# Another order of the seven products of the down projection in a one-core encoder block, with the last norm and the outputs set elsewhere in it

## The chip, the cores and the metric

The kernel runs on one core of a Trainium2 chip. The metric is the device time of one execution in microseconds, from the hardware. The time before is the median of three runs.

## What is computed

One block of a streaming encoder on 1024 frames and 16 meta tokens, model width 1024, float32. A mixer (retention and forgetting attention) is followed by a gated feed-forward part and a last RMS norm. What matters here is the end:

```python
up = h @ w_up                       # 1024 -> 2 * 2816
a, b = split(up)
u = silu(causal_conv(a)) * b        # 1024 tokens x 2816
h = h + u @ w_down                  # 2816 -> 1024
out = h * rsqrt(mean(h * h) + 1e-6) * final_norm_g
```

The mean goes over the 1024 features of a token; the 16 meta tokens are dropped from the output.

## The kernel before

The state is kept transposed: features on the 128 partitions, tokens in the free dimension. Every float32 matrix product is done as three fp32r products of split operands (high by high, high by low, low by high).

**The down product.** `u @ w_down` is done by Strassen's scheme in Winograd's form: features of w_down, of u and the tokens are cut in two, and seven products of half size take the place of eight. `DSEQ` (L1391) names the pair of operands of each: the products with index i = 0 to 6 are A11·B11, S2·T2, A12·B21, S3·T3, S1·T1, A22·T4, S4·B22. A are quarters of w_down, B quarters of u (B11 and B12 are the first 1408 features of u for the first and the last 512 tokens), S and T sums of them, formed while the up product runs and kept in device memory (`wS`, `uT`, `uB` in the profile's rows). The inner size 1408 is 11 tiles of 128, so that a product is 11 **steps** (`KH` = 11); a step is 4 blocks of 128 output features, 3 matmuls each, of 512 tokens: 12 matmuls. The loop variable g = 0 to 76 counts the steps, g // 11 is the place of the product and g % 11 (`kt`) its step.

**Units.** A step needs two units (`d_unit`, L1415): one tile 128x512 of each operand, loaded by SP's queue (`d_load`, L1400: `d_raw`), cast to fp32r on ScalarE (L1262) and subtracted on VectorE (L1263) for the low half (`d_u`). The program writes the units of step g + 4 behind the matmuls of step g; twelve unit buffers hold six steps.

**Sums.** The products with index 0, 2, 4, 6 collect in four PSUM banks X (`psa`, `psc`), those with index 1, 3, 5 in four banks Y (`psb`, `psx`). A bank goes on accumulating from one product of its group to the next, apart from index 4, which starts anew. After each product `d_post` (L1645) adds the banks to the residual H (8 tiles of 128 features by 1024 tokens; a half of the tokens at a time): index 0 by four ScalarE copies and twelve GpSimd adds (L1651, L1653), the others by four VectorE adds that read PSUM (L1656). H comes back from device memory by eight loads during the first product (L1723). The post of a product is written behind the first step of the next.

**Last norm and outputs.** `FCH` cuts the tokens into chunk 0 (the first 512), chunk 1 and chunk 2 (256 each). `sq_add` (L1661) squares a tile of H on ScalarE and adds it to `ac`; `f_norm` (L1674) sums over partitions by matmuls with a column of ones (`nps`, L1679), takes the root (L1681), the reciprocal (L1682), scales unit matrices with it (`dg`, L1686) and spreads it over all partitions by a matmul with a matrix of ones (`pr`, L1687). `f_emit` (L1695) writes an output tile `fo`: either ScalarE scales by the norm's gain (L1705) and GpSimd multiplies by a copy `prs` of the factor (L1706), or VectorE does both and reads `pr` from PSUM (L1708). In the last product the first 8 steps are whole, and the last three (`NL` = 3) run by halves of 256 tokens, all four blocks of the first half and then of the second, so that chunk 1 can be finished before chunk 2.

The first 512 tokens are complete only with index 5, the sixth product; the seventh completes the last 512 for the first four feature tiles. The four computing engines run in the order in which the program is written (a manual schedule); the order of SP's DMA issues comes from the scheduler.

## Time and profile before

| | us |
|---|---|
| median of the three runs (1322.06 to 1330.04) | 1327.36 |
| the profiled execution | 1325.43 |
| its span, first to last instruction | 1323.6 |
| TensorE busy, share of the span | 1267.7 (96%) |
| VectorE, ScalarE, GpSimd busy | 920.3, 588.7, 376.7 |
| HBM read, written | 132.59 MB, 52.21 MB |

The profile comes from one execution, and all sums below are made on it. A row of a timeline gives the start from the span's begin, the time from the first to the last of the merged instructions, the engine, the line, the tiles and how many there were. PE is TensorE, PEld its weight loads, DVE VectorE, ACT ScalarE, POOL GpSimd, SP the engine that issues the DMAs. Busy TensorE is not the same as TensorE at its peak, since matmuls overlap and their ends are modelled.

### The profile page before, as it was taken

The numbers are of one execution on the slowest core, as the hardware profiler recorded it, in microseconds if no ns is written. First come the engines' busy times: TensorE is split into PE (matmuls) and PEld (weight loads), VectorE is DVE, ScalarE is ACT, GpSimd is POOL, SyncE is SP. The second block draws the span as 40 slices with busy tenths as digits, with TensorE's granted clock in tenths as the row PEclk, the third lists the DMA queues.
The fourth block names the chain that finished last, engine by engine and source line by source line (L and its number), as shares of the span: only waits on it lengthen the run. The fifth ranks groups of instructions, "written<-read, shape, count | busy, mean of one in ns | idle before, by whom it ended". The sixth has DMA issues, their size and how long they took to land.

```text
span 1323.6 us, 24163 instructions
## 1 busy us (share of the span) xinstructions
PE 1267.7 (96%) x9243; PEld 1198.8 (91%) x9243; DVE 920.3 (70%) x1573; ACT 588.7 (44%) x1162; POOL 376.7 (28%) x308
## 2 busy tenths in 40 slices
PE   8999999999999999988799999999999999999995
PEld 8999999999999889977699999999999997888884
DVE  5776546556657655747877877878989885855566
ACT  7773442455454554434243343343333435444553
POOL 0154144000000000033344644645645531400123
PEclk9999999999999999988799999999999998999998
DMA  8532125114213553264145535437557579666633
GB/s 281 177 96 90 32 67 130 33 50 116 72 50 101 158 157 102 88 199 144 35 135 158 159 120 160 159 121 223 180 180 226 177 240 349 243 200 193 197 105 126
DMA packets 110946, 192.75 MB, mean 146 GB/s; under 512 B 15143, under 2 KB 50295, under 8 KB 110832
## 3 DMA queue, kind: packets, MB, share of 16 engines
q1 hardware_dynamic: 110832, 191.23, 45.8%
q8 instruction: 72, 1.18, 0.4%
q14 instruction: 42, 0.34, 0.1%
HBM read 132.59 MB, written 52.21 MB: 140 GB/s over the span
## 4 chain that ended last, share of the span: by engine, by line
PE 81%; DVE 8%; DMA 4%; ACT 3%; issue 2%; POOL 1%; SPq 1%; DVEq 0%; ACTq 0%; POOLq 0%
PE psb L1287 14%; PE psD L666 11%; PE psc L1287 9%; PE psa L1287 9%; PE psO L824 4%; PE psc L1438 4%; PE psa L1438 4%; PE psD L894 3%; PE psx L1438 3%; PE psb L1438 3%; PE psS L787 3%; PE psS L730 2%; PE psj L183 2%; PE psj L185 2%; PE psj L184 2%
## 5 line engine op out<-in xcount | busy, mean ns | idle before, releaser
L1263 DVE TENSOR_TENSOR d_u<-d_raw,d_u 128x512 fp32r<-128x512 f32 x154 | 118.6, 823 | 61.5 <-ACT d_u L1262 61.5
L1262 ACT CAST d_u<-d_raw 128x512 fp32r<-128x512 f32 x154 | 87.3, 619 | 98.7 <-PE psc L1438 48.5
L666 PE MATMUL psD<-xl,f_hi 128*128 128x256 f32 (+2 forms) x448 | 129.9, 290 | 0.0
L666 PE MATMUL psD<-xh,f_hi 128*128 128x256 f32 (+2 forms) x448 | 129.0, 288 | 0.4 <-DVE fq L672 0.4
L666 PE MATMUL psD<-xh,f_lo 128*128 128x256 f32 (+2 forms) x448 | 128.8, 287 | 0.0
L1258 POOL TENSOR_TENSOR S<-u_raw 128x512 f32<-128x512 f32 x44 | 64.0, 1456 | 196.7 <-DVE unit L1263 194.9
L1287 PE MATMUL psb<-B1T,unit 128*128 128x256 f32 x780 | 103.2, 282 | 4.2 <-DVE at L1303 4.2
L1287 PE MATMUL psb<-B0T,unit 128*128 128x256 f32 x780 | 104.3, 283 | 0.0
L1287 PEld LDWEIGHTS psb<-B1T,unit 128*128 128x128 f32 x780 | 97.4, 191 | 4.4 <-ACT B1T L1150 4.4
L797 ACT ACTIVATE pf<-psS 128x272 f32<-128x272 f32 (+4 forms) x112 | 49.6, 450 | 114.2 <-PE psS L787 69.9
L1287 PEld LDWEIGHTS psb<-B0T,unit 128*128 128x128 f32 x780 | 98.2, 191 | 0.0
L1262 ACT CAST unit<-S 128x512 fp32r<-128x512 f32 x87 | 54.2, 622 | 78.2 <-PE psb L1287 75.7
L1263 DVE TENSOR_TENSOR unit<-S,unit 128x512 fp32r<-128x512 f32 x87 | 81.0, 931 | 8.2 <-ACT unit L1262 8.2
L666 PEld LDWEIGHTS psD<-xh,f_hi 128*128 128x128 f32 x448 | 85.4, 191 | 0.9 <-DVE fq L672 0.6
L666 PEld LDWEIGHTS psD<-xl,f_hi 128*128 128x128 f32 x448 | 85.2, 190 | 0.4
L666 PEld LDWEIGHTS psD<-xh,f_lo 128*128 128x128 f32 x448 | 85.2, 190 | 0.1
L1444 POOL MEMSET on<- 128x128 f32 x1 | 0.2, 204 | 297.2 <-PE psS L791 297.2
L733 DVE TENSOR_REDUCE mx<-psS 128x1 f32<-128x512 f32 (+6 forms) x120 | 59.0, 539 | 30.2 <-PE psS L730 20.9
L183 PE MATMUL psj<-rv_hi,xh 128*128 128x256 f32 (+1 forms) x264 | 75.6, 290 | 1.9 <-ACT rv_hi L117 1.1
L184 PE MATMUL psj<-rv_lo,xh 128*128 128x256 f32 (+1 forms) x264 | 74.8, 285 | 0.3 <-DVE rv_lo L118 0.3
L185 PE MATMUL psj<-rv_hi,xl 128*128 128x256 f32 (+1 forms) x264 | 74.7, 286 | 0.1
L1438 PE MATMUL psa<-d_u 128*128 128x512 f32 (+1 forms) x282 | 69.2, 383 | 5.0 <-DVE d_u L1263 3.9
(343 smaller groups left out, 3559.8 us busy)
## 6 DMA issues: line engine op xcount, KB each, us to landing
u_raw<-wup SPq DMA_DIRECT2D x44, 512.0 KB
sd<-wdn SPq DMA_DIRECT2D x88, 128.0 KB
uB<-u SPq DMA_DIRECT2D x44, 256.0 KB
wS<-sd SPq DMA_DIRECT2D x88, 128.0 KB
d_raw<-wS SPq DMA_DIRECT2D x44, 256.0 KB
d_raw<-uT SPq DMA_DIRECT2D x44, 256.0 KB
d_raw<-wdn SPq DMA_DIRECT2D x33, 256.0 KB
d_raw<-uB SPq DMA_DIRECT2D x33, 256.0 KB
```

Of the source, the lines that this page charges most:

```text
L183: pe.matmul(ps[:, :w], lhsT=x_h, rhs=w_h[:, c0:c0 + w], start=(k == 0), stop=False)
L184: pe.matmul(ps[:, :w], lhsT=x_h, rhs=w_l[:, c0:c0 + w], start=False, stop=False)
L185: pe.matmul(ps[:, :w], lhsT=x_l, rhs=w_h[:, c0:c0 + w], start=False, stop=(k == KT - 1))
L666: pe.matmul(ps[:, :n], lhsT=w_, rhs=X(e, k, t0 + a, n), start=(k == 0 and i == 0), stop=(k == KT - 1 and i == 2))
L733: dve.tensor_reduce(mxs[s][:R - q_, j, ci:ci + 1], ps[:R - q_, :n], axis=mybir.AxisListType.X, op=ALU.max)
L797: act.activation(pf[:r, a:b], ps[:r, a:b], AF.Exp)
L824: pe.matmul(po[:, q0 - qs:qn], lhsT=v_, rhs=P2[:r, P_, off:off + n], start=(i == 0 and e == 0), stop=(fin and e == 2))
L1258: pool.tensor_tensor(t, s_[x], s_[y], op=o)
L1262: act.copy(t[:, 0], src)
L1263: eng.tensor_tensor(t[:, 1], src, f(t[:, 0]), op=ALU.subtract)
L1287: pe.matmul(ps[:, :n], lhsT=w[:, wi, k * P:(k + 1) * P], rhs=o[:, hl, k, :], start=(new and k == 0 and j == 0), stop=(k == 3 and j == 2), ...
L1438: pe.matmul(ps[:, c:c + n], lhsT=a_[:, wi, j * P:(j + 1) * P], rhs=b_[:, hl, c:c + n], start=(new and m == 0), stop=(kt == KH - 1 and m == ...
```

## The change

- `DORD` sets another order of the products: by index 1, 0, 3, 2, 5, 4, 6. The first 512 tokens are now complete after the fifth product. The sixth and the seventh product are both of group X, so the banks that index 4 leaves are read by `d_post(4, j)` at the seam, and this is now written ahead of block j of the first step of the seventh product.
- The norm of chunk 0 is worked out within the sixth product (column sums behind its step 6, root and `dg` behind step 8, spreading behind step 9), and its eight output tiles are written in the seventh, one a step, all by VectorE from PSUM. Before, ScalarE and GpSimd wrote seven of them.
- The last five steps run by halves instead of three. The norm of chunk 1 comes in two pieces behind blocks 0 and 1 of the second half.
- Other engines: `dg` mostly on ScalarE; the last square of chunks 1 and 2 is not added to `ac` but goes into the column sums as a second matmul; output tiles 4 to 7 of chunk 1 and 4 to 6 of chunk 2 are scaled early by ScalarE (`f_pre`) and multiplied by GpSimd, the others are VectorE's; the last two tiles of chunk 2 are stored by a DMA of their own each.

```diff
--- before.py
+++ after.py
...
     DSEQ = (("A11", "B11"), ("S2", "T2"), ("A12", "B21"), ("S3", "T3"), ("S1", "T1"), ("A22", "T4"), ("S4", "B22"))
+    DORD = (1, 0, 3, 2, 5, 4, 6)
     d_raw, d_units, d_next, d_two, d_last = {}, {}, [0], [None], [None]
...
     def d_load(g):
         if g < 7 * KH and g not in d_raw:
-            i, kt = divmod(g, KH)
+            i, kt = DORD[g // KH], g % KH
             if g < 2:
...
     X = Y = None
     def d_mm(g, j, c, n, new):
-        i, kt = divmod(g, KH)
+        i, kt = DORD[g // KH], g % KH
         a_, b_ = d_units[g, 0], d_units[g, 1]
...
             else:
                 sq = es.tile([P, 512], F32, tag="sq4", name="sq4", bufs=4)[:, :n]
                 act.activation(sq, hsl, AF.Square)
-                (pool if ci == 0 else dve).tensor_tensor(acs[ci], acs[ci], sq, op=ALU.add)
-        prd = {}
-        def f_norm(ci):
+                if ci and d == 3:
+                    acs[ci + 2] = sq
+                else:
+                    (pool if ci == 0 and d < 4 else dve).tensor_tensor(acs[ci], acs[ci], sq, op=ALU.add)
+        dgd, prd, fo = {}, {}, {}
+        def f_nps(ci):
             c0, n = FCH[ci]
             m = n // P
             ps = (pb, px)[ci % 2].tile([P, 512], F32, tag=("psb", "psx")[ci % 2], name="nps")
+            src = [acs[ci]] + ([acs[ci + 2]] if ci else [])
             for j in range(m):
-                pe.matmul(ps[:, j:j + 1], lhsT=acs[ci][:, j * P:(j + 1) * P], rhs=ones, start=True, stop=True)
+                for x, a_ in enumerate(src):
+                    pe.matmul(ps[:, j:j + 1], lhsT=a_[:, j * P:(j + 1) * P], rhs=ones,
+                              start=(x == 0), stop=(x == len(src) - 1))
+            prd[ci] = ps
+        def f_dg(ci):
+            m = FCH[ci][1] // P
             r = es.tile([P, 4], F32, tag="fr", name="fr", bufs=3)[:, :m]
-            act.activation(r, ps[:, :m], AF.Sqrt, bias=epsc, scale=1.0 / 1024)
+            act.activation(r, prd[ci][:, :m], AF.Sqrt, bias=epsc, scale=1.0 / 1024)
             dve.reciprocal(r, r)
-            pr = (pb, px)[ci % 2].tile([P, 512], F32, tag=("psb", "psx")[ci % 2], name="pr")[:, :n]
+            dgd[ci] = []
             for j in range(m):
                 dg = es.tile([P, P], F32, tag="dg", name="dg", bufs=4)
-                dve.tensor_scalar(dg, idf, r[:, j:j + 1], None, op0=ALU.mult)
+                if ci == 2 and j == 0:
+                    dve.tensor_scalar(dg, idf, r[:, j:j + 1], None, op0=ALU.mult)
+                else:
+                    act.activation(dg, idf, AF.Copy, scale=r[:, j:j + 1])
+                dgd[ci].append(dg)
+        def f_bc(ci):
+            c0, n = FCH[ci]
+            pr = (pb, px)[ci % 2].tile([P, 512], F32, tag=("psb", "psx")[ci % 2], name="pr")[:, :n]
+            for j, dg in enumerate(dgd[ci]):
                 pe.matmul(pr[:, j * P:(j + 1) * P], lhsT=on, rhs=dg, start=True, stop=True)
             prd[ci] = [pr, None]
-            if OUTE[ci]:
+            if ci:
                 prd[ci][1] = es.tile([P, n], F32, name=f"prs{ci}")
                 act.copy(prd[ci][1], pr)
-        fo = {}
-        def f_emit(ci, d):
+        def f_out(ci, d):
+            m = 512 // FCH[ci][1]
+            if (ci, d - d % m) not in fo:
+                fo[ci, d - d % m] = [es.tile([P, m, FCH[ci][1]], F32, tag="fo", name="fo", bufs=8), 0]
+            return fo[ci, d - d % m]
+        def f_pre(ci, d):
             c0, n = FCH[ci]
-            pr, prs = prd[ci]
+            act.activation(f_out(ci, d)[0][:, d % 2, :], H[d][:, c0:c0 + n], AF.Copy, scale=sm[:, S_LG + d:S_LG + d + 1])
+        def f_emit(ci, d, pre=False):
+            c0, n = FCH[ci]
             m = 512 // n
-            if d % m == 0:
-                fo[ci] = es.tile([P, m, n], F32, tag="fo", name="fo", bufs=8)
-            ot = fo[ci][:, d % m, :]
-            hsl = H[d][:, c0:c0 + n]
-            g = sm[:, S_LG + d:S_LG + d + 1]
-            if OUTE[ci] & (1 << d):
-                act.activation(ot, hsl, AF.Copy, scale=g)
-                pool.tensor_tensor(ot, ot, prs, op=ALU.mult)
+            t = f_out(ci, d)
+            ot = t[0][:, d % m, :]
+            if pre:
+                pool.tensor_tensor(ot, ot, prd[ci][1], op=ALU.mult)
             else:
-                dve.scalar_tensor_tensor(ot, hsl, g, pr, op0=ALU.mult, op1=ALU.mult)
-            if d % m == m - 1:
-                sp.dma_start(out[(d + 1 - m) * P:(d + 1) * P, c0:c0 + n].rearrange("(a p) n -> p a n", p=P), fo[ci])
-        NL = 3
+                dve.scalar_tensor_tensor(ot, H[d][:, c0:c0 + n], sm[:, S_LG + d:S_LG + d + 1], prd[ci][0],
+                                         op0=ALU.mult, op1=ALU.mult)
+            t[1] += 1
+            if ci == 2 and d > 5:
+                sp.dma_start(out[d * P:(d + 1) * P, c0:c0 + n], ot)
+            elif t[1] == m:
+                d0 = d - d % m
+                sp.dma_start(out[d0 * P:(d0 + m) * P, c0:c0 + n].rearrange("(a p) n -> p a n", p=P), t[0])
+        NL = 5
         for g in range(7 * KH):
-            i, kt = divmod(g, KH)
-            if i < 6 or kt < KH - NL:
+            pos, kt = divmod(g, KH)
+            if pos < 6 or kt < KH - NL:
                 for j in range(4):
-                    d_mm(g, j, 0, 512, i in (0, 1, 4) and kt == 0)
-            if i and kt == 0:
+                    if pos == 6 and kt == 0:
+                        d_post(4, j)
+                    d_mm(g, j, 0, 512, DORD[pos] in (0, 1, 4) and kt == 0)
+            if 0 < pos < 6 and kt == 0:
                 for j in range(4):
-                    d_post(i - 1, j)
-            if i == 0 and 2 <= kt < KT + 2:
+                    d_post(DORD[pos - 1], j)
+            if pos == 0 and 2 <= kt < KT + 2:
                 with tc.issue_after(d_last[0].ins):
                     sp.dma_start(H[kt - 2], hsave[kt - 2][:, 2:])
-            if i == 1 and kt == 4:
+            if pos == 2 and kt == 4:
                 wz.close()
                 es = mk(do, "es")
                 on = es.tile([P, P], F32, name="on2")
                 pool.memset(on, 1.0)
-            if i == 5 and 2 <= kt < 10:
-                if kt < 6:
-                    sq_add(0, kt - 2)
-                elif kt < 10:
-                    sq_add(1, kt - 2)
-                    sq_add(2, kt - 2)
-            if i == 6:
-                if kt in (1, 2):
-                    sq_add(0, 2 + 2 * kt)
-                    sq_add(0, 3 + 2 * kt)
-                if kt == 3:
-                    f_norm(0)
-                if 4 <= kt < 8:
-                    f_emit(0, 2 * kt - 8)
-                    f_emit(0, 2 * kt - 7)
+            if pos == 4 and 2 <= kt < 6:
+                sq_add(0, kt - 2)
+            if pos == 5:
+                if 1 <= kt < 5:
+                    sq_add(0, 3 + kt)
+                if kt == 6:
+                    f_nps(0)
+                if kt == 8:
+                    f_dg(0)
+                if kt == 9:
+                    f_bc(0)
+            if pos == 6:
+                if kt < 4:
+                    sq_add(1, 4 + kt)
+                    sq_add(2, 4 + kt)
+                if kt < KT:
+                    f_emit(0, kt)
             for _ in range(3):
                 if d_next[0] < 2 * (g + 5):
                     d_unit()
+        for d in range(4, KT):
+            f_pre(1, d)
         for hf in range(2):
...
                 hsl = H[j][:, 512 + 256 * hf:768 + 256 * hf]
                 dve.tensor_tensor(hsl, X[j][:, 256 * hf:256 * hf + 256], hsl, op=ALU.add)
+                if hf and j == 0:
+                    f_nps(1)
+                    f_dg(1)
+                if hf and j == 1:
+                    f_bc(1)
+                    for d in range(4, KT):
+                        f_emit(1, d, True)
                 sq_add(1 + hf, j)
-                if hf and j == 1:
-                    f_norm(1)
-        for d in range(KT):
-            f_emit(1, d)
-        f_norm(2)
-        for d in range(KT):
+                if hf and j == 2:
+                    f_emit(1, 0)
+                    f_emit(1, 1)
+                if hf and j < 3:
+                    f_pre(2, 4 + j)
+        f_emit(1, 2)
+        f_emit(1, 3)
+        f_nps(2)
+        f_dg(2)
+        f_bc(2)
+        for d in (4, 5, 6):
+            f_emit(2, d, True)
+        for d in (0, 1, 2, 3, 7):
             f_emit(2, d)
```

How the rows move: first TensorE in the last product, before (the first row ends its fourth step; `psa` and `psc` are the banks X):

```order
L1438 MATMUL psc<-d_u 128x512 x6
L1679 MATMUL nps<-ones,ac_15100 128x1 x4
L1687 MATMUL pr<-dg,on_14200 128x128 x4
L1438 MATMUL psa<-d_u 128x512 x6
...
L1438 MATMUL psa<-d_u 128x256 x18
L1438 MATMUL psc<-d_u 128x256 x18
...
L1679 MATMUL nps<-ones,ac_15195 128x1 x2
L1687 MATMUL pr<-dg,on_14200 128x128 x2
L1438 MATMUL psc<-d_u 128x256 x18
L1679 MATMUL nps<-ones,ac_15197 128x1 x2
L1687 MATMUL pr<-dg,on_14200 128x128 x2
```

and the same engine after, from the halves on:

```order
L1439 MATMUL psa<-d_u 128x256 x30
L1439 MATMUL psc<-d_u 128x256 x30
L1439 MATMUL psa<-d_u 128x256 x15
L1685 MATMUL nps<-ones,ac_15337 128x1
L1685 MATMUL nps<-ones,sq_15567 128x1
...
L1439 MATMUL psa<-d_u 128x256 x15
L1707 MATMUL pr<-dg,on_14435 128x128 x2
L1439 MATMUL psc<-d_u 128x256 x30
...
L1685 MATMUL nps<-ones,sq_15674 128x1
...
L1707 MATMUL pr<-dg,on_14435 128x128 x2
```

Before, column sums and spreading of chunk 0 stand next to each other inside the last product, as do those of chunk 1; now chunk 0's have left the last product, chunk 1's are 15 matmuls apart, and the halves hold 120 matmuls in place of 72.

VectorE in the last product, after, from the seam (the four adds of `d_post(4, j)`) into its second step and from the last units on:

```order
L1657 TENSOR_TENSOR H_13814<-psc,H_13814 128x512
L1731 SCALAR_TENSOR_TENSOR fo<-H_13811,sm,pr 128x512
L1263 TENSOR_TENSOR d_u<-d_raw,d_u 128x512 x2
L1674 TENSOR_TENSOR ac_15337<-ac_15337,sq_15365 128x256
L1674 TENSOR_TENSOR ac_15339<-ac_15339,sq_15368 128x256
L1731 SCALAR_TENSOR_TENSOR fo<-H_13812,sm,pr 128x512
...
L1674 TENSOR_TENSOR ac_15339<-ac_15339,sq_15649 128x256
L1731 SCALAR_TENSOR_TENSOR fo<-H_13811,sm,pr 128x256
L1731 SCALAR_TENSOR_TENSOR fo<-H_13812,sm,pr 128x256
L1786 TENSOR_TENSOR H_13814<-psc,H_13814 128x256
L1731 SCALAR_TENSOR_TENSOR fo<-H_13813,sm,pr 128x256
```

Every step of the last product now carries an output tile, and in four of them two adds of squares, ahead of the two units; near the end two output tiles of chunk 1 stand ahead of the last add to H (L1786), where seven stood behind it before.

SP at the start of the first product, after (`wS` and `uT` are S2 and T2 of its last step, `hs` the saved H):

```order
L1356 DMA uT_7593<-T2o 128x512
L1356 DMA uT_7594<-T3o 128x512
L1356 DMA uT_7595<-T4o 128x512
L1414 DMA d_raw<-uT_7593 128x512
L1753 DMA H_13811<-hs_7573 128x1024
L1753 DMA H_13812<-hs_7574 128x1024
```

Before, the store of T2 and the load of it were eleven steps apart and the first two loads of H stood ahead of that store; now the load follows right behind the three stores and the loads of H stand behind it.

## Rows read from the trace of the kernel before

**Rows 1.** The stretches of the seven products and of the end: busy time of each engine with its instructions in brackets, granted TensorE clock, DMA share and GB/s.
```profile
1095.00:1122.60 27.60, 27.12 (x108) 22.23 (x109) 15.34 (x25) 13.21 (x24) 1.33 (x2) 0.89 0.92 339
...
1242.30:1272.20 29.90, 29.90 (x133) 24.75 (x133) 18.79 (x33) 18.36 (x36) 4.37 (x4) 1.00 0.59 194
1272.20:1310.50 38.30, 33.97 (x193) 29.39 (x191) 25.69 (x39) 17.43 (x34) 17.25 (x11) 1.00 0.18 69
1310.50:1323.60 13.10, 1.85 (x8) 1.53 (x8) 6.82 (x19) 2.25 (x6) 2.14 (x3) 0.58 0.47 160
```

**Rows 2.** Waits in the seventh product: who waited for whom, us in total, times, longest.
```profile
ACT fr L1681 <- PE nps L1679: 6.5, 1, 6.5
...
PE pr L1687 <- DVE dg L1686: 3.3, 2, 2.4
...
PE psa L1438 <- DVE d_u L1263: 1.0, 1, 1.0
```

**Rows 3.** The chain that ended last, in the seventh product: start, us, engine, tile and line. A step of twelve matmuls is two such rows, of `psa` and `psc`; the rows left out are the rest of the first four steps.
```profile
1272.21 1.36 PE psa L1438 x6
...
1283.09 0.80 PE nps L1679 x8
...
1284.77 1.17 PE pr L1687 x8
```

**Rows 4.** TensorE's timeline of the halves at the end of the seventh product, in brackets idle time before the instruction and what ended it.
```profile
1296.69 0.99 PE L1438 MATMUL psa<-d_u 128*128 128x256 f32 x7
1298.69 1.58 PE L1438 MATMUL psa<-d_u 128*128 128x256 f32 x11 [1.01 <-DVE d_u L1263]
1300.11 2.32 PE L1438 MATMUL psc<-d_u 128*128 128x256 f32 x18
1302.27 2.32 PE L1438 MATMUL psa<-d_u 128*128 128x256 f32 x18
1304.60 0.61 PE L1679 MATMUL nps<-ones,ac 128*128 128x1 f32 x4
1307.60 0.71 PE L1687 MATMUL pr<-dg,on 128*128 128x128 f32 x4 [2.39 <-DVE dg L1686]
1308.07 2.40 PE L1438 MATMUL psc<-d_u 128*128 128x256 f32 x18
```

**Rows 5.** VectorE in the sixth product, where GpSimd does nothing at the time: how long units, adds of squares and adds to H take one behind the other.
```profile
1260.52 0.75 DVE L1670 TENSOR_TENSOR ac<-ac,sq 128x256 f32<-128x256 f32 x2
...
1267.46 1.29 DVE L1263 TENSOR_TENSOR d_u<-d_raw,d_u 128x512 fp32r<-128x512 f32 x2 [1.43 <-ACT d_u L1262]
1270.21 1.37 DVE L1656 TENSOR_TENSOR H<-psb,H 128x512 f32<-128x512 f32 x2 [1.45 <-PE psb L1438]
```

**Rows 6.** Groups by shape, from the first product to the end: busy us, mean ns of one, idle time before.
```profile
L1263 DVE TENSOR_TENSOR d_u<-d_raw,d_u 128x512 fp32r<-128x512 f32 x150 | 115.0, 820 | 61.5 <-ACT d_u L1262 61.5
L1708 DVE SCALAR_TENSOR_TENSOR fo<-H,sm,pr 128x512 f32<-128x512 f32 x1 | 0.7, 734 | 0.0
L1686 DVE TENSOR_SCALAR dg<-idf,fr 128x128 f32<-128x128 f32 x8 | 1.8, 284 | 0.1
L1706 POOL TENSOR_TENSOR fo<-fo,prs 128x256 f32<-128x256 f32 x3 | 2.1, 729 | 17.0 <-ACT fo L1705 17.0
```

**Rows 7.** Groups by shape at 1291.5 to 1293.0, where GpSimd multiplies output tiles.
```profile
L1263 DVE TENSOR_TENSOR d_u<-d_raw,d_u 128x512 fp32r<-128x512 f32 x2 | 3.5, 1782 | 0.0
L1706 POOL TENSOR_TENSOR fo<-fo,prs 128x512 f32<-128x512 f32 x2 | 3.5, 1743 | 0.0
```

**Rows 8.** The end: rows of the timelines of the engines from the last matmuls of the product, put in order of time; rows beside this chain are left out.
```profile
1309.83 0.64 PE L1438 MATMUL psc<-d_u 128*128 128x256 f32 x4
1310.74 0.42 DVE L1752 TENSOR_TENSOR H<-psc,H 128x256 f32<-128x256 f32 x1
1311.25 0.42 ACT L1669 ACTIVATE sq<-H 128x256 f32<-128x256 f32 x1 [0.89 <-DVE H L1752]
1312.04 2.83 DVE L1708 SCALAR_TENSOR_TENSOR fo<-H,sm,pr 128x256 f32<-128x256 f32 x7
1312.27 0.66 PE L1679 MATMUL nps<-ones,ac 128*128 128x1 f32 x4 [1.81 <-DVE ac L1670]
1312.97 0.26 ACT L1681 ACTIVATE fr<-nps,epsc 128x2 f32<-128x2 f32 x1 [0.91 <-PE nps L1679]
1314.78 0.16 DVE L1682 RECIPROCAL fr<-fr 128x2 f32<-128x2 f32 x1
1314.98 0.48 DVE L1686 TENSOR_SCALAR dg<-idf,fr 128x128 f32<-128x128 f32 x2
1315.41 1.19 PE L1687 MATMUL pr<-dg,on 128*128 128x128 f32 x4 [2.48 <-DVE dg L1686]
1316.64 0.37 ACT L1691 COPY prs<-pr 128x256 f32<-128x256 f32 x1 [3.41 <-PE pr L1687]
1317.10 2.44 DVE L1708 SCALAR_TENSOR_TENSOR fo<-H,sm,pr 128x256 f32<-128x256 f32 x6 [1.64 <-issue]
```

**Rows 9.** SP's issues around the first product (no row has landing times).
```profile
1098.29 0.32 SPq L1356 DMA_DIRECT2D uT<-T2o  x1
...
1106.18 0.32 SPq L1413 DMA_DIRECT2D d_raw<-wS  x1
...
1120.56 0.32 SPq L1723 DMA_DIRECT2D H<-hs  x1
```

## The prediction

> **What bounds the kernel now.** I read the stretches first [rows 1]. From the second to the sixth product a stretch takes 29.9 us and TensorE is busy for all of it (the sixth: 29.90 of 29.90); eleven steps of 2.72 us, two rows of 1.36 each [rows 3], are 29.92. Nothing that spares VectorE, ScalarE or GpSimd there buys time. The first product has 0.48 us of idle TensorE. The seventh takes 38.30 us with 33.97 busy, and behind it lie 13.10 us with hardly a matmul, at a granted clock of 0.58. So the change can work on some 51 us, and what it can give is what the seventh product and the end lose.
>
> What the seventh loses: it begins at 1272.21 [rows 3] and its last matmul ends at 1308.07 + 2.40 = 1310.47 [rows 4], 38.26 us. Eight whole steps are 21.76. Eighteen matmuls of 256 tokens take 2.16 (1300.11 to 1302.27 [rows 4]), 0.12 each; the 72 of the halves are 8.64. Together 30.40; 7.86 us are lost. The waits [rows 2] and the places [rows 3, 4] name them: column sums 0.80 and spreading 1.17 of chunk 0, with 0.9 of waiting for `dg` between; 1.01 for late units; 3.47 from 1304.60 to 1308.07 for chunk 1's norm, 2.39 of it a wait for `dg`; the rest is ends of pipelines. The late units come from two things: ScalarE stands 6.5 us in front of the root [rows 2], with the casts behind it, and a unit's subtraction takes 1.78 us while GpSimd multiplies [rows 7], against some 0.645 when it does not (two in 1.29 [rows 5]).
>
> The end [rows 8]: from 1310.47 the last add to H, square, add, sums, root; the reciprocal waits behind seven output tiles (1312.04 + 2.83) until 1314.78, though the root was done at 1313.23; then `dg`, spreading, copy, six tiles until 1319.54, and 4.06 us of stores to the span's end at 1323.6: 13.13 us.
>
> **The change, part by part.**
>
> *Order of the products.* The same 77 steps; TensorE's count does not change. The post of index 0 (12 GpSimd adds, 4 ScalarE copies) moves from the second into the third product, against units of the same kind and lead: nothing. VectorE's post of index 1 moves from the third to the second, where GpSimd is now idle: nothing. *SP's queue* is passed by loads: S2 and T2 now belong to the first product, and the load of the last T2 stands right behind its store, ahead of all loads of H. The queue blocks until that store has landed. The store is issued at about 1098.3 and the next loads before went out at 1106.18 [rows 9], for want of a free buffer, so up to 7.9 us of block cost nothing; the first step that needs this T2 is the eleventh, ten steps or 27 us after the product began. H moves later by two loads, and 0.92 of DMA time is busy [rows 1]: bounds 0 and, if H is late by as much as those 7.9 us, a few us of VectorE, covered by the units' lead of four steps (10.9 us). I take 0.
>
> *The seam.* The sixth and seventh product now share banks. Block j of the seventh may begin when its bank has been read. A block lasts 0.68 us, so a bank is done 2.04 us before it is wanted again; hand-over and add take 0.27 (1310.47 to 1310.74 [rows 8]) + 0.69 (1.37 for two [rows 5]) = 0.96. Bounds 0 and, if VectorE comes late by a whole step, 2.7. VectorE was busy 18.79 of 29.90 in the sixth [rows 1]; four adds for chunk 0 join it. I take 0.
>
> *Norm of chunk 0.* Its matmuls go into the sixth product: the same 1.97 us, without the waits, as root and `dg` stand two steps ahead of their users.
>
> *Units in the seventh.* This is where I see the risk. VectorE starts with the last post, at 0.96 us after the seam. Step 1: output tile 0.73 [rows 6] and two units 1.29; steps 2 to 4 two adds 0.75 more; steps 5 to 7 without. 0.96 + 2.02 + 3 x 2.77 + 3 x 2.02 = 17.35 us for the last unit. TensorE wants it after six whole steps, 16.32, and twelve matmuls of the first half block, 1.44: at 17.76. It holds by 0.4 us if GpSimd stays idle, which it does in this stretch. With the mean over all units, 0.820 [rows 6], the 14 units take 2.45 more and TensorE waits 2.0; at 1.78 [rows 7] 15.5. I take 0.2, the value without GpSimd and some hand-overs.
>
> That output tiles now read PSUM is spoken against by a rule: the Trainium skill, VectorE: DVE Perf Modes, Rules for kernel authors, advises copying a matmul's output to SBUF first if many operations will read it. The rows give 0.734 for the PSUM form and 0.687 as the least for two SBUF inputs, 0.05 for each of the seven tiles ahead of the last unit: by the rule the sum would be some 0.2 us lower, a wait that I put at 0.2 anyway.
>
> *The halves.* Six whole steps 16.32, 120 matmuls of 256 at 0.12 make 14.40; against 21.76 + 8.64 that is 0.32 more. Chunk 1's norm: four sums 0.80 (chunk 0's four [rows 3]) and spreading 0.71 [rows 4]; its root, reciprocal and `dg` lie beside a block of 1.8 us. End of the pipeline 0.24.
>
> Sum from the seam: 1.97 + 16.32 + 14.40 + 1.51 + 0.24 + 0.2 = 34.64, against 38.26: **3.6 us less**.
>
> *The end.* From the last matmul: add to H 0.69; square 0.09 + 0.42; sums 0.14 + 0.80; root 0.04 + 0.26; reciprocal 0.15 + 0.16; `dg` 0.04 + 0.30 (ScalarE's form is not in the trace; bounds 0.26 and 0.37, its root and its copy [rows 8]); spreading 0.13 + 1.19; copy 0.41; five tiles at 0.41 and a hand-over 2.12; stores 4.06: 11.0. GpSimd's three tiles, 0.73 each [rows 6], end about with VectorE's. To this comes a queue on VectorE: an add of squares and two tiles of chunk 1 stand ahead of the last add to H, and GpSimd multiplies chunk 1's tiles next to them. The block before ends 1.8 us ahead of the last; add, square, add of squares and tiles end at -1.80 + 0.69 + 0.51 + 0.05 + x + 0.82, where H could go at 0.27. x is not in the trace: 0.37 alone [rows 5], or a whole GpSimd tile more, 1.10. The queue costs 0.4 or 1.1; I take 0.9, since GpSimd's four tiles run for 2.9 us just there. The end is 11.9 against 13.13: **1.2 us less**. Bounds of it: 0 and 2.4, if the smaller last stores land earlier too.
>
> On x the Trainium skill, SBUF — State Buffer, Who interferes with whom, says that a VectorE instruction with two SBUF inputs and a GpSimd one that reads SBUF shut each other out for a whole instruction. The 1.78 beside 1.74 agrees; by it x is 1.1 and the sum 0.2 us worse than mine.
>
> **The sum.** 3.6 + 1.2 = 4.8 us. The profiled execution, 1325.43 with a span of 1323.6, would go to 1320.6; it lay 1.9 under the median of the runs shown. Off the median: **1322.6 us**, 0.36% faster. A measurement here can tell 0.5%, 6.6 us, from no change, so this is within it.
>
> **The rivals.**
> 1. *The gain is larger.* GpSimd leaves the add alone, no unit is late, the two last stores of half size end sooner: 3.8 + 2.4, and with another 1 us from waits that I cannot see (the ends of pipelines in the 7.86) 7.2: 1320.2. For it: the idle time of the reciprocal, 1.55, vanishes whole. Against it: x.
> 2. *VectorE bounds the seventh product, a little.* The units at 0.82, wait 2.0, the end with x at 1.1: 4.8 - 1.8 - 0.2 = 2.8 down to 0: 1324.6 to 1327.4. For it: a margin of 0.4 in 17.8 us. Against it: GpSimd is what made them slow.
> 3. *VectorE bounds it outright: slower.* The last five steps want five units' worth within one block; where before the last unit was wanted after eight whole steps, it is now wanted 4.9 us sooner. If something keeps a unit at 1.78, the wait is 15.5 and the time 1322.6 + 15.3 = 1337.9. It breaks even with the kernel before at a wait of 5.0, a mean unit of (17.76 + 5.0 - 17.35) / 14 + 0.645 = 1.03 us. Against it: only squares, tiles and units run there, none on GpSimd.
> 4. *The first product starves.* SP's block behind the store holds loads of units and of H. Beyond the 7.9 us each us is a us once the lead of 10.9 is used up; 10 us more would give 1322.6 + 7 = 1330. Against it: ten steps of time.
>
> **How the numbers follow.** Forecast (gain 3 to 6.6) 0.55; larger 0.22; a little late 0.15; outright late 0.05; starved 0.03. Faster by over 0.5% takes the larger gain and some of the forecast that three runs scattered over 8 us may carry there: 0.30. Slower by over 0.5% is the outright case and a part of the last: 0.06. Within: 0.64. The range goes from the larger gain with x at its least and the scatter of a median, 1316.5, to the little-late case, 1328; the others are left out.
>
> **What would show it.** Right: the stretch of the sixth product about 2 us longer and still wholly busy; 66 steps without a wait; from the seam to the last matmul 32.7 us; no wait for `dg` inside the product; from the last matmul to the end about 12. The unit step is wrong if TensorE waits for `d_u` by over 1 us in the first half block; the seam, if it waits for H at the seventh product's first step; x, if the last add to H begins over 1.5 us behind the last matmul. The forecast is wrong if the time does not fall below 1328 or falls under 1316.5.

## The result

| | kernel before | changed kernel |
|---|---|---|
| median | 1323.58 us (20 runs, 1318.84 to 1334.32) | 1316.12 us (20 runs, 1311.79 to 1326.02) |
| ratio of the times | | 0.995, 95% interval 0.9931 to 0.9969 |
| profiled execution, span | 1325.43, 1323.6 us | 1326.02, 1323.9 us |

The changed kernel is 6.6 us faster by the ratio (4.1 to 9.1), 0.5%; the two medians lie 7.5 us apart. The interval leaves out 1, so the gain is clear of the scatter, and its size is just what the prediction called the least that can be told. The forecast was 4.8 us.

The two profiled spans are equal all the same. The changed kernel's profiled execution was the slowest of its 20, and it lost its time ahead of the change: the down product's first matmul stands at 1085.34 in the profile before and at 1091.73 after, and in the nine profiles of the experiments below anywhere from 1079.24 to 1095.24, although none of these kernels changes the work ahead of it, but for the operands that the first loads fetch. So times scatter by several us, and a part of the kernel is better compared by its length within a profile. I use three lengths: from the down product's first matmul to the seam (the start of the seventh product), from the seam to the end of the last matmul, and from there to the end of the span. In the profile before, the seam is the start of this row:
```profile
1272.05 1.52 PE L1438 MATMUL psa<-d_u 128*128 128x512 f32 x6
```
The prediction took 1272.21, from the chain of [rows 3]. A row of the chain begins where the row before it ends, 0.16 us behind the start of its first matmul, so the prediction's 38.26 us for the seventh product is 0.16 short.

| | to the seam | seam to last matmul | end | sum |
|---|---|---|---|---|
| before | 186.71 | 38.42 | 13.13 | 238.26 |
| changed | 188.25 | 32.20 | 11.72 | 232.17 |

The sum is 6.09 us shorter, which agrees with the times.

**Up to the seam.** Two things alone set this length apart between kernels. One is chunk 0's norm, 1.86 us, which the change puts there (the sixth product takes 31.78 us from its first matmul at 1248.20, less 29.92). The other is the granted clock in the first product. In all eleven profiles TensorE waits about 1.17 and 2.87 us in the third step, and the matmuls behind the second wait run at the lower level. Before, the first five of them and the stretch of the first eleven (columns as in [rows 1]):
```profile
1095.48 2.50 PE L1438 MATMUL psa<-d_u 128*128 128x512 f32 x5 [2.87 <-DVE d_u L1263]
```
```profile
1095.48:1100.34 4.86, 4.86 (x11) 3.80 (x12) 1.75 (x3) 0.00 (x0) 0.00 (x0) 0.50 1.05 388
```
The clock comes up again within the next six. These 17 matmuls take 6.57 us before, 6.24 after, and up to 6.80 in the runs below. Less them and the norm, the part up to the seam is 180.14 to 180.17 us in all eleven kernels. So the order of the products costs nothing there, and 0.3 of the 6.09 us is this clock, which differs as much between kernels whose first product is the same.

**The profile after.** The stretches of the sixth product, of the seventh up to the halves, of the halves, and of the end (columns as in [rows 1]):
```profile
1248.37:1279.98 31.61, 31.61 (x148) 26.40 (x148) 19.07 (x32) 16.84 (x32) 0.00 (x0) 1.00 0.59 184
1279.98:1296.31 16.33, 16.33 (x74) 13.52 (x73) 16.33 (x30) 10.66 (x24) 0.00 (x0) 1.00 0.40 145
1296.31:1312.18 15.87, 15.87 (x133) 15.67 (x131) 6.60 (x15) 5.46 (x15) 3.01 (x4) 1.00 0.08 29
1312.18:1323.90 11.72, 2.38 (x13) 1.97 (x12) 4.59 (x13) 1.45 (x4) 2.09 (x3) 0.62 0.47 164
```
TensorE is busy for the whole of the first three stretches, at a granted clock of 1.00 (the level of 2.4 GHz). VectorE is busy for the whole of 1279.98 to 1296.31 as well: that is the load on which the prediction hung.

TensorE's waits from 1120 us to the end, in the same form as [rows 2]:
```profile
PE nps L1685 <- ACT sq L1670: 1.2, 1, 1.2
PE pr L1707 <- DVE dg L1698: 1.0, 1, 1.0
PE nps L1685 <- DVE ac L1674: 0.3, 1, 0.3
```
All three lie behind the last matmul of the product. The waits of [rows 2] are gone: none for `dg` inside the product, none for a unit.

TensorE's timeline of the halves, against [rows 4]:
```profile
1296.31 3.76 PE L1439 MATMUL psa<-d_u 128*128 128x256 f32 x30
...
1303.50 1.96 PE L1439 MATMUL psa<-d_u 128*128 128x256 f32 x15
1305.30 0.28 PE L1685 MATMUL nps<-ones,ac 128*128 128x1 f32 x2
...
1306.11 2.04 PE L1439 MATMUL psa<-d_u 128*128 128x256 f32 x15
1307.98 0.61 PE L1707 MATMUL pr<-dg,on 128*128 128x128 f32 x4
1308.35 3.83 PE L1439 MATMUL psc<-d_u 128*128 128x256 f32 x30
```
Sums (1305.30 to 1306.11) and spreading (1307.98 to 1308.35) of chunk 1 stand between blocks without a wait; root, reciprocal and `dg` ran during the block at 1306.11.

VectorE in the seventh product and at the end, against [rows 5, 8]:
```profile
1281.45 1.29 DVE L1263 TENSOR_TENSOR d_u<-d_raw,d_u 128x512 fp32r<-128x512 f32 x2
1282.65 0.76 DVE L1674 TENSOR_TENSOR ac<-ac,sq 128x256 f32<-128x256 f32 x2
...
1285.19 0.75 DVE L1674 TENSOR_TENSOR ac<-ac,sq 128x256 f32<-128x256 f32 x2
...
1292.12 0.74 DVE L1731 SCALAR_TENSOR_TENSOR fo<-H,sm,pr 128x512 f32<-128x512 f32 x1
...
1293.98 0.74 DVE L1731 SCALAR_TENSOR_TENSOR fo<-H,sm,pr 128x512 f32<-128x512 f32 x1
1294.64 1.28 DVE L1263 TENSOR_TENSOR d_u<-d_raw,d_u 128x512 fp32r<-128x512 f32 x2
...
1309.36 0.74 DVE L1674 TENSOR_TENSOR ac<-ac,sq 128x256 f32<-128x256 f32 x1 [0.74 <-ACT sq L1670]
...
1311.39 0.98 DVE L1674 TENSOR_TENSOR ac<-ac,sq 128x256 f32<-128x256 f32 x1 [0.54 <-ACT sq L1670]
1312.30 0.86 DVE L1731 SCALAR_TENSOR_TENSOR fo<-H,sm,pr 128x256 f32<-128x256 f32 x2
1313.08 0.41 DVE L1786 TENSOR_TENSOR H<-psc,H 128x256 f32<-128x256 f32 x1
```
and GpSimd beside it:
```profile
1309.08 3.01 POOL L1729 TENSOR_TENSOR fo<-fo,prs 128x256 f32<-128x256 f32 x4 [79.29 <-ACT prs L1711]
```
Every pair of units takes 1.28 or 1.29; a step of VectorE takes 2.54 with the adds of squares (1282.65 to 1285.19) and 1.86 without (1292.12 to 1293.98); the last unit is done at 1295.92, 15.94 us behind the seam. Beside GpSimd's four tiles (1309.08 to 1312.09) the last two adds of squares take 0.74 and 0.98, and the last add to H starts 0.90 behind the last matmul.

### The profile page after: what moved, and what is told of

Its sections match the earlier page's. It is cut to its first block, busy times and chain, and to the rows that moved or that the text cites. A ratio compares the mean times of both kernels' runs of the same rounds, so it can differ in the third digit from the quotient of the medians.

```text
span 1323.9 us, 24222 instructions
## 1 busy us (share of the span) xinstructions
PE 1271.6 (96%) x9275; PEld 1204.6 (91%) x9275; DVE 926.7 (70%) x1571; ACT 588.1 (44%) x1165; POOL 363.2 (27%) x301
## 4 chain that ended last, share of the span: by engine, by line
PE 78%; DVE 8%; DMA 5%; issue 4%; ACT 3%; POOL 1%; SPq 1%; POOLq 0%; DVEq 0%; ACTq 0%
PE psb L1287 13%; PE psD L666 10%; PE psc L1287 9%; PE psa L1287 9%; PE psO L824 4%; PE psD L894 4%; PE psa L1439 3%; PE psc L1439 3%; PE psx L1439 3%; PE psb L1439 3%; PE psS L787 3%; PE psj L183 2%; PE psj L185 2%; PE psj L184 2%; PE psS L730 2%
## 5 line engine op out<-in xcount | busy, mean ns | idle before, releaser
L1263 DVE TENSOR_TENSOR d_u<-d_raw,d_u 128x512 fp32r<-128x512 f32 x154 | 109.4, 762 | 57.2 <-ACT d_u L1262 57.2
L1287 PE MATMUL psa<-B0B,unit 128*128 128x258 f32 x516 | 69.9, 285 | 0.0
```

Source lines behind the costliest of these rows:

```text
L1263: eng.tensor_tensor(t[:, 1], src, f(t[:, 0]), op=ALU.subtract)
L1287: pe.matmul(ps[:, :n], lhsT=w[:, wi, k * P:(k + 1) * P], rhs=o[:, hl, k, :], start=(new and k == 0 and j == 0), stop=(k == 3 and j == 2), ...
```

## The experiments

**What holds the units and the matmuls up: four runs.** First, the norm of chunk 0 late again: it leaves the sixth product for the seventh.
```diff
-                if kt == 6:
-                    f_nps(0)
-                if kt == 8:
-                    f_dg(0)
-                if kt == 9:
-                    f_bc(0)
...
-                if kt < KT:
-                    f_emit(0, kt)
+                if kt == 3:
+                    f_nps(0)
+                    f_dg(0)
+                    f_bc(0)
+                if 4 <= kt < 8:
+                    f_emit(0, 2 * kt - 8)
+                    f_emit(0, 2 * kt - 7)
```


> The changed kernel, but the norm of chunk 0 (sums, root, dg, spreading) again behind the fourth step of the seventh product, and its eight output tiles two to a step behind that. Theory (the gain of the seventh product is the root and dg taken out of TensorE's way, and units no longer held up behind them): TensorE waits 1.0 to 1.6 us for dg inside the product; the reciprocal holds VectorE's queue until 12 us after the seam, so the last unit is done at about 22.4 us after it, where TensorE wants it at 20.8, which adds a wait for d_u of about 1.6. Seam to last matmul: the 32.2 us of the changed kernel + 1.7 of sums and spreading moved back in + 1.3 + 1.6 = 36.8; against the changed kernel 2.9 us slower in sum, since the sixth product gets its 1.7 back. Rival (only the direct wait counts; VectorE has the same work in both, so units are on time): 1.3 slower, no wait for d_u. The end from the last matmul stays 11.7 by both.

Measured: 1322.32 us, ratio to before 0.9987 (0.9962 to 1.0012). Lengths 186.95, 37.52, 11.69 (in the order of the table). Between seam and last matmul that is 5.3 us more than in the changed kernel; 1.86 of it came over from the sixth product, so 3.5 us are lost, where theory said 2.9 and the rival 1.3. (The sums of the lengths differ by 4.0, but 0.55 of that is the clock in the first product.) The wait for `dg` is 1.09; but the wait for a unit only 0.34, and another cost stands there that neither had. The stretches of the sums with the spreading, and of the first step behind them:
```profile
1277.07:1280.37 3.30, 2.21 (x18) 2.15 (x16) 0.18 (x1) 2.07 (x7) 0.00 (x0) 0.91 0.00 0
1280.37:1283.07 2.70, 2.70 (x8) 2.12 (x8) 2.68 (x5) 2.58 (x5) 0.00 (x0) 0.50 0.02 6
```
Behind the wait the granted clock is 0.50 (the level of 1.2 GHz): a row of six matmuls takes 2.70 in place of 1.36. That is 1.34 us that neither theory had, and it also gave VectorE time, so that the unit was less late. The direction was right, the division was not.

To tell the pause from the rest, the same kernel with a shorter one:
```diff
-                if ci == 2 and j == 0:
+                if ci == 0 or ci == 2 and j == 0:
                     dve.tensor_scalar(dg, idf, r[:, j:j + 1], None, op0=ALU.mult)
```


> The run with chunk 0's norm late, but its four dg made by VectorE as in the kernel before in place of ScalarE. In the late-norm run TensorE waited 1.09 us for dg, the spreading took 1.60 in place of 1.05, and in the 2.70 us behind it the granted clock was 0.50; in the kernel before it waited 0.89, and the clock stayed at 1.00. Theory (the lower clock follows from the longer wait and the slow spreading, one dg after the other): the wait is 0.9, the spreading 1.15, the clock stays at 1.00, and seam to last matmul is 35.6 to 36.0 in place of 37.5. Rival (the clock falls behind any such pause in this kernel, or for a reason that lies elsewhere): about 1.3 us of half clock again, 37.3.

Measured: 1319.55 us, ratio 0.9953 (0.9937 to 0.9970). Lengths 186.91, 36.47, 11.16. TensorE's rows around the spreading, and the wait for a unit later:
```profile
1281.95 0.95 PE L1685 MATMUL nps<-ones,ac 128*128 128x1 f32 x8
1283.88 1.13 PE L1707 MATMUL pr<-dg,on 128*128 128x128 f32 x8 [0.98 <-DVE dg L1698]
1284.76 1.62 PE L1439 MATMUL psa<-d_u 128*128 128x512 f32 x6
1286.22 1.52 PE L1439 MATMUL psc<-d_u 128*128 128x512 f32 x6
...
1293.13 2.29 PE L1439 MATMUL psa<-d_u 128*128 128x256 f32 x17 [1.12 <-DVE d_u L1263]
```
The row behind the spreading lasts 1.46 until the next, and the clock is at its upper level, as the theory had it. That the shorter wait is the reason is not shown: there is one profile of each kernel, the waits differ by 0.11 us, and the kernel before kept its clock behind 2.39 [rows 4]. With TensorE earlier by that much, the unit is late by 1.12, which is most of the 1.6 that the late-norm run had been expected to show. That is 0.78 more than in the late-norm run, and by so much 36.47 lies above the expectation's 35.6 to 36.0. The times can't tell this kernel from the changed one (0.9953 and 0.995). By the lengths the place of chunk 0's norm is worth 4.27 us between seam and last matmul (36.47 - 32.20), of which 1.86 is work that went into the sixth product: 2.4 of gain, and 1 us more where the clock falls.

Third, GpSimd back at chunk 0's tiles, all else as changed:
```diff
-            if ci:
+            if True:
                 prd[ci][1] = es.tile([P, n], F32, name=f"prs{ci}")
                 act.copy(prd[ci][1], pr)
...
                 if kt < KT:
-                    f_emit(0, kt)
+                    f_pre(0, kt)
+                    f_emit(0, kt, True)
```
The first part is the copy of the spread roots that GpSimd needs; it stands on ScalarE in the sixth product. `f_pre` scales on ScalarE, `f_emit` with `True` multiplies on GpSimd.

> The changed kernel, but the eight output tiles of chunk 0 in the seventh product made by ScalarE (copy with gain) and GpSimd (multiply) in place of VectorE, in the same places. VectorE has 7 x 0.73 us less to do before the last unit. Theory (a unit beside a GpSimd multiply takes 1.5 to 1.8 us in place of 0.645): about 14 us of multiplies; the last unit done at some 21 us after the seam where 17.8 is wanted, TensorE waits 3 us for d_u (1 to 5), seam to last matmul 35.2 in place of 32.2. Rival (what counts is VectorE's number of instructions, and GpSimd takes work off it): last unit done at about 12.5 us after the seam, no wait, seam to last matmul 32.2, time unchanged.

Measured: 1322.65 us, ratio 0.9986 (0.9964 to 1.0008). Lengths 188.55, 38.10, 10.67 (TensorE waits at the seam here; it is put at 1272.13, where the sixth product's matmuls hand over): 5.9 us more between seam and last matmul, where 3 was expected and the rival had 0. The waits of TensorE there:
```profile
PE psa L1439 <- DVE d_u L1263: 1.9, 3, 1.0
PE psa L1439 <- DVE H L1657: 1.6, 1, 1.6
```
VectorE's units, four ahead of GpSimd's work and two pairs in it:
```profile
1270.74 2.50 DVE L1263 TENSOR_TENSOR d_u<-d_raw,d_u 128x512 fp32r<-128x512 f32 x4 [6.73 <-ACT d_u L1262]
...
1279.44 2.38 DVE L1263 TENSOR_TENSOR d_u<-d_raw,d_u 128x512 fp32r<-128x512 f32 x2
...
1282.42 3.48 DVE L1263 TENSOR_TENSOR d_u<-d_raw,d_u 128x512 fp32r<-128x512 f32 x2
```
Pairs of units take 2.38 and 3.48 beside GpSimd where they take 1.25 without (four in 2.50): the theory holds, and VectorE with fewer instructions was later. Its last unit was done 22.6 us behind the seam (1294.71), 6.6 later than in the changed kernel. But not all of that is GpSimd's: the first row shows a second way to be late. VectorE was idle for 6.73 us ahead of it, since ScalarE had the copy of the spread roots in its queue and waited for them for 6.40, with the units' casts behind it:
```profile
1269.60 0.59 ACT L1711 COPY prs<-pr 128x512 f32<-128x512 f32 x1 [6.40 <-PE pr L1707]
1270.08 2.18 ACT L1262 CAST d_u<-d_raw 128x512 fp32r<-128x512 f32 x4
```
So VectorE came to the adds to H of the seam 2.9 us later than in the changed kernel (1273.15 is 1.02 behind the seam, 1278.14 was 1.84 ahead of it), and TensorE waited 1.60 at the first block of the seventh product. The other 3.8 of the 6.6 us arose beside GpSimd, with seven tiles fewer on VectorE. Of the 5.9 us, the waits are 3.5. Of the rest, 2.4 us, about half is seen in one place behind them: 17 matmuls from 1294.76 on took 3.18 at a granted 0.62, at 0.12 each 2.04.

Fourth, one part of the change alone in the kernel before: its chunk 0 tiles by VectorE.
```diff
-OUTE = [127, 8, 66]
+OUTE = [0, 8, 66]
```


> The kernel before, with one edit: the eight output tiles of chunk 0 all by VectorE from the spread roots, none by ScalarE and GpSimd, in the same places (two to a step). Theory (units are late for two reasons: ScalarE's casts stand behind the root until 1286.4, and GpSimd's multiplies stretch the subtractions): only the second is taken away; from 1286.4 on four pairs of units take 5.2 and six tiles 4.4 us, the last unit is done at about 1296.6 by the clock of the profile before, where TensorE wants it at 1297.7. The 1.01 us of waiting for d_u vanish, the waits for dg stay: seam to last matmul 37.2 in place of 38.26, 1.0 us faster than the kernel before, the end 13.1 as before. Rival (VectorE, not GpSimd, is what is short: six more tiles of 0.73 come ahead of the last unit): the wait for d_u grows to 2 us or more and the time with it.

Measured: 1323.69 us, ratio 0.9994 (0.9968 to 1.0019). Lengths 186.89, 38.53, 13.17. The wait for units is gone, as the theory had it; from the seam to the end of the third half block it is 31.27 us, against 32.55 before. The edit also takes seven scalings and a copy off ScalarE; but VectorE was busy without a gap with the six units from 1289.36 on in the profile before, 9.28 us for three pairs, where each pair takes 1.28 now, so it was the stretching that went. Yet nothing is gained to the last matmul:
```profile
1307.57 0.61 PE L1679 MATMUL nps<-ones,ac 128*128 128x1 f32 x4
1310.58 1.22 PE L1687 MATMUL pr<-dg,on 128*128 128x128 f32 x4 [2.40 <-DVE dg L1686]
1311.45 3.38 PE L1438 MATMUL psc<-d_u 128*128 128x256 f32 x18
```
The same wait as in [rows 4], 2.40 for 2.39, and behind it 3.38 in place of 2.40 for the same eighteen matmuls, and 1.22 in place of 0.71 for the spreading. The stretch from 1310.58 to the last matmul has a granted clock of 0.63. The 1.3 us gained were given back behind that wait, at the lower clock.

**The number of halves: two runs.** Five in the kernel before, alone:
```diff
-        NL = 3
+        NL = 5
```


> The kernel before, with one edit: five last steps by halves in place of three. Theory (there the units are set by VectorE beside GpSimd's multiplies, not by when TensorE asks): the last unit is done at the same 26.4 us after the seam (1298.6), TensorE wants it at 20.6 and waits 5.8 in place of 1.01 for d_u; then 108 matmuls of 256 (12.96) and chunk 1's norm 3.47: seam to last matmul 43.2 in place of 38.26, 4.9 us slower than the kernel before (3 to 6). Rival (units come when TensorE needs them, as they do in the changed kernel with the same five): 0.3 slower or a little faster, wait for d_u about 1.

Measured: 1330.32 us, ratio 1.0047 (1.0030 to 1.0064): slower. Lengths 186.94, 45.47, 12.99: 7.0 us more between seam and last matmul than before, where 4.9 was expected.
```profile
1293.56 0.62 PE L1438 MATMUL psa<-d_u 128*128 128x256 f32 x3 [2.66 <-DVE d_u L1263]
1296.91 4.00 PE L1438 MATMUL psa<-d_u 128*128 128x256 f32 x17 [2.73 <-DVE d_u L1263]
...
1310.03 0.71 PE L1687 MATMUL pr<-dg,on 128*128 128x128 f32 x4 [1.54 <-DVE dg L1686]
1310.50 5.31 PE L1438 MATMUL psc<-d_u 128*128 128x256 f32 x30
```
The waits for units are 5.39 (5.8 expected). The clock adds 3.2 us to them: 17 matmuls in 3.80 until the next row, at a granted clock of 0.50, where 17 at 0.12 take 2.04, and 30 in 5.31, at 0.68, where the changed kernel takes 3.83. Without the other parts of the change the five halves are the third rival of the prediction in a mild form.

Three in the changed kernel:
```diff
-        NL = 5
+        NL = 3
```


> The changed kernel with three instead of five last steps by halves. Theory (five steps make a block long enough to hide root and dg of chunk 1, and give VectorE's queue time before the last add to H): 0.32 us are saved in the halves; dg comes 1.55 us behind the sums (1306.02 to 1307.57 in the profile of the changed kernel) where the block lasts 1.08, a wait of 0.5; the last add to H starts 1.9 us behind the last matmul in place of 0.9, the end is 12.7 in place of 11.7. In sum 1.2 us slower (0.8 to 1.6). Rival (a shorter last part is simply shorter): 0.3 faster, end 11.7.

Measured: 1318.76 us, ratio 0.9957 (0.9937 to 0.9976). Lengths 188.43, 32.69, 13.08: 0.49 more in the product, 1.36 more in the end, 1.85 in sum (1.2 expected, 1.6 at most); the rival is out, the size was too small.
```profile
1302.96 0.38 PE L1685 MATMUL nps<-ones,sq 128*128 128x1 f32 x2 [0.46 <-ACT sq L1670]
...
1308.80 0.35 PE L1685 MATMUL nps<-ones,ac 128*128 128x1 f32 x2 [1.09 <-DVE ac L1674]
```
Shorter blocks leave the sums waiting for a square (0.46), not the spreading for `dg`; behind the last matmul the sums wait for an add of squares 1.09 in place of 0.34. Its last add to H started 1.64 us behind the last matmul, 1.9 expected. That delay is 0.75 of the 1.36; another 0.6 is the last six column sums, which took 1.43 at a granted clock of 0.50 where they take 0.83 at 1.00 in the changed kernel. The theory did not have this.

**The end: three runs.** The end depends on the clock too: the spreading of chunk 2 takes 1.19 us at a granted 0.50 in the changed kernel, and 0.68 at 1.00 in the late-norm run with VectorE's `dg` and in the run with GpSimd's tiles, whose ends are shorter by at least that. It is 1.11 to 1.19 in the three runs here. The last add to H ahead of chunk 1's tiles:
```diff
-                if hf and j == 2:
-                    f_emit(1, 0)
-                    f_emit(1, 1)
...
-        f_emit(1, 2)
-        f_emit(1, 3)
+        for d in range(4):
+            f_emit(1, d)
```


> The changed kernel, but the two output tiles of chunk 1 that stand ahead of VectorE's last add to H are moved behind it, so that four stand there. Theory (the queue on VectorE is a term of the end): the last add to H starts about 0.3 us behind the last matmul in place of 0.90; add and four tiles end 2.4 behind it, the root is done at about 2.4, so the reciprocal is not held up; the end from the last matmul is 10.7 to 11.1 us in place of 11.72, 0.6 to 1.0 us faster, too little for the time alone (ratio to the changed kernel 0.9992 to 0.9995) and to be read from the profile. Rival (the tiles are paid in any place, as in the kernel before, where seven stood ahead of the reciprocal): the reciprocal waits and the end stays at 11.7.

Measured: 1318.14 us, ratio 0.9943 (0.9915 to 0.9971), not to be told from the changed kernel by the time. Lengths 188.48, 32.20, 10.82: the end is 0.90 shorter, 0.08 of it in the spreading.
```profile
1307.09 0.98 DVE L1674 TENSOR_TENSOR ac<-ac,sq 128x256 f32<-128x256 f32 x1 [0.54 <-ACT sq L1670]
1307.99 0.41 DVE L1786 TENSOR_TENSOR H<-psc,H 128x256 f32<-128x256 f32 x1
1308.32 1.64 DVE L1731 SCALAR_TENSOR_TENSOR fo<-H,sm,pr 128x256 f32<-128x256 f32 x4
1310.12 0.17 DVE L1693 RECIPROCAL fr<-fr 128x2 f32<-128x2 f32 x1 [0.16 <-ACT fr L1692]
```
The add starts 0.11 behind the last matmul (1307.88), and the reciprocal waits for the root, not for the tiles. The queue is a term of the end, and this order is better than that of the change.

The same, with GpSimd's tiles later too:
```diff
-            if ci:
-                prd[ci][1] = es.tile([P, n], F32, name=f"prs{ci}")
-                act.copy(prd[ci][1], pr)
+            if ci == 2:
+                f_prs(2)
+
+        def f_prs(ci):
+            prd[ci][1] = es.tile([P, FCH[ci][1]], F32, name=f"prs{ci}")
+            act.copy(prd[ci][1], prd[ci][0])
...
-                    for d in range(4, KT):
-                        f_emit(1, d, True)
...
-                if hf and j == 2:
-                    f_emit(1, 0)
-                    f_emit(1, 1)
...
-        f_emit(1, 2)
-        f_emit(1, 3)
+        f_prs(1)
+        for d in range(4, KT):
+            f_emit(1, d, True)
+        for d in range(4):
+            f_emit(1, d)
```


> As the run with the last add to H moved first, and the copy of chunk 1's spread roots behind the last square on ScalarE, so that GpSimd's four tiles of chunk 1 start about 1.3 us behind the last matmul and no add of squares runs beside them. Theory (an add of squares is stretched by a multiply of GpSimd that it meets: 0.74 and 0.98 in the changed kernel, 0.43 alone): both adds of squares in the last two blocks take 0.43; the last add to H starts 0.27 behind the last matmul, the end is 10.7. GpSimd's four tiles end about 4.3 behind the last matmul, before its three last ones begin at about 4.9. Rival (the stretch depends on which VectorE instruction meets the multiply; then it passes to those that now do): reciprocal, dg or tiles of chunk 1 take up to 0.7 more each and the end is 11 to 12.

Measured: 1318.55 us, ratio 0.9942 (0.9913 to 0.9971). Lengths 188.42, 32.21, 11.68: the end is not 10.7.
```profile
1306.82 0.43 DVE L1674 TENSOR_TENSOR ac<-ac,sq 128x256 f32<-128x256 f32 x1 [0.54 <-ACT sq L1670]
1307.65 0.42 DVE L1789 TENSOR_TENSOR H<-psc,H 128x256 f32<-128x256 f32 x1 [0.41 <-PE psc L1439]
1308.88 1.66 DVE L1734 SCALAR_TENSOR_TENSOR fo<-H,sm,pr 128x256 f32<-128x256 f32 x4 [0.80 <-ACT prs L1714]
1310.45 0.16 DVE L1693 RECIPROCAL fr<-fr 128x2 f32<-128x2 f32 x1
1310.64 0.45 DVE L1698 TENSOR_SCALAR dg<-idf,fr 128x128 f32<-128x128 f32 x1
```
The adds of squares take 0.43 with GpSimd out of the way, which was the theory. What I had missed: VectorE's tiles, which read the same spread roots, stood behind ScalarE's copy of them and started only after it (0.80 of waiting). The reciprocal stands behind the tiles, and `dg` beside GpSimd takes 0.45 in place of 0.29. The gain was spent by a wait that my edit made, and a little by the rival.

The last two tiles in one store:
```diff
-            if ci == 2 and d > 5:
-                sp.dma_start(out[d * P:(d + 1) * P, c0:c0 + n], ot)
-            elif t[1] == m:
+            if t[1] == m:
```


> The changed kernel with the last two tiles stored in one transfer of 256 KB in place of two of 128 KB. Theory (the smaller last stores give nothing: from the last tile to the span's end the kernel before took 4.06 us, the changed one 4.3): the end from the last matmul stays within 0.3 us of 11.72. Rival (half the bytes land earlier): it grows by up to 1.2.

Measured: 1329.79 us, a single execution, so only the lengths count: 188.62, 32.20, 11.54. The end is 0.18 shorter than that of the changed kernel, within the 0.3 expected, and it did not grow as the rival had it. By these two profiles the smaller last stores give nothing.

## Why the prediction was right, and where its sizes were off

*The time.* The gain was forecast as 4.8 us, "3 to 6.6", and measured as 6.6 by the ratio, at the end of that. The median of the twenty runs after, 1316.12, lies under 1316.5, which the prediction named as a sign of being wrong. But its range was counted from 1327.36, the median of three runs before, and twenty put that at 1323.58; the measured ratio off 1327.36 gives 1320.7. Of the 6.5 us from 1322.6 to 1316.12, 3.8 are that start, and 2.7 a gain forecast too small (7.5 by the medians for 4.8).

*What bounds the kernel* held for the change: up to the seam only the moved norm and the clock of the first product differ between the kernels, and all else was decided in the last 51 us. One reading was wrong. "The first product has 0.48 us of idle TensorE" comes from a stretch that begins at 1095.00 [rows 1], 9.7 us behind that product's first matmul (1085.34). From there to the second product at 1122.45 it is 37.11 us, where eleven steps are 29.92: 7.2 us are lost, to the two waits in its third step (4.04) and the lower clock behind them. That is nearly what the seventh product lost, and it still stands in the changed kernel (36.80). No term of the sum rests on it, but whoever looks for the next gain would not find it in the prediction's 51 us.

*Order of the products, SP's queue, the fourth rival.* Taken as 0, and 0: no wait of TensorE from the fourth step of the first product to the seam. SP's queue did block, and for less than the 7.9 us that the prediction allowed: the store of the last T2 was issued at 1101.46 and the load of it at 1107.60, with 3.2 us of waiting for the store. The last load of H came no later: it was issued 35.17 us behind the down product's first matmul, 35.22 before [rows 9].

*The seam.* 0, as taken. The run with GpSimd's tiles shows what is lost there when ScalarE's queue holds back the units and VectorE's adds with them: 1.60, of a bound of 2.7.

*Norm of chunk 0.* It was put at 1.97 in the sixth product and took 1.86.

*Units.* This step was right in kind and too careful in size: forecast 17.35 us after the seam for the last unit, 15.94 measured; wanted at 17.76. I had added up busy times, but neighbouring instructions overlap by some 0.07: a step took 2.54 and not 2.77, or 1.86 and not 2.02, which makes 1.3 of the 1.4; the rest is the start: VectorE went on from the seam's adds to its first tile at 0.81 instead of 0.96. So the margin was 1.8, and the 0.2 of waiting that I took did not come. That GpSimd and not VectorE's count sets the pace was the choice on which the forecast stood. Two runs confirm it: with GpSimd's tiles a pair took up to 3.48, and with VectorE's tiles in the kernel before it took 1.28 and no unit was late, though VectorE had six more tiles ahead of the last unit. The rule of the Trainium skill (VectorE: DVE Perf Modes, Rules for kernel authors), to copy a matmul's output to SBUF first if many operations follow, had nothing to gain here: the tiles took 0.74 from PSUM, and no wait was there to shorten. No run has VectorE read them from SBUF, and the prediction's 0.687 for that stands in none of its rows.

*The halves.* 120 matmuls and 16.32 us of whole steps came as counted. Spreading was priced by its busy time, 0.71; TensorE lost 0.37, as the next block's matmuls follow before the row ends. From the seam 32.20 in place of the 32.7 announced.

*The end.* 11.72 for 11.9. The add of squares that the prediction called x was 0.98, near the upper of its two ends, but the block before it ended and was handed over some 0.3 sooner than I had it, so the queue cost 0.6 and not 0.9: two errors that partly cancel. The Trainium skill (SBUF — State Buffer, Who interferes with whom) says that a VectorE instruction with two SBUF inputs and a GpSimd one that reads SBUF shut each other out for a whole instruction; 0.98 here agrees, but the run with chunk 0's tiles on GpSimd has an add of squares of 0.43 at 1309.43 amid GpSimd's four tiles (1307.17 to 1310.45), so VectorE does not pay it each time. The smaller stores gave nothing, so that bound fell away.

*The sum.* In the seventh product 6.22 less the 1.86 of the moved norm, 4.4; in the end 1.4; in the first product's clock 0.3: 6.1 in place of 3.6 + 1.2 = 4.8. Of the 1.3 missing, 0.2 are the units, 0.3 the spreading, 0.1 the moved norm, 0.2 the seam read 0.16 late, 0.3 the clock in the first product, 0.2 the end. The first rival, with a gain of 7.2, was nearer than the forecast, by the profiles (1.1 off against 1.3) and by the ratio of the times (0.6 against 1.8). But of its three reasons only one, no late unit, came true: GpSimd did not leave the add alone, and the smaller stores ended no sooner.

*What no run takes apart.* Of the 4.4 us in the seventh product, 2.4 are shown by the run that moves chunk 0's norm. No run puts the two pieces of chunk 1's norm together again, and none takes the new order of the products alone. That the wait of 2.39 for `dg` went because a block now stands between sums and spreading is read from the rows, and so is that the reciprocal of chunk 2 no longer stands behind seven tiles (1.55 of the end).

*What the prediction did not have:* the clock. It priced each wait at its length. In the seventh product of the profile before, the clock stayed at 1.00 up to the last matmul; but the sign stood in [rows 1], 0.89 for the first product, where eleven matmuls behind a wait took 4.86 us at 0.50. In four of the nine other kernels waits in the seventh product were followed by matmuls at or near the lower level, for 1 to 3 us more. The changed kernel has no wait in its seventh product, and its clock was 1.00 there. Whether that is why the times differ by a little more (6.6 by the ratio) than the two profiles (6.1) stays open: it lies within the interval.
